# A hybrid block on one core: the front in three groups instead of two, with selection issued between mixing, and other limits for the sparse gathers

## The chip, the cores and the metric

The kernel runs on one core of a Trainium2 chip. The metric is the device time of one execution in microseconds; less is better. Five engines work beside each other, each in the order of its own instruction stream: TensorE (PE; its weight loads are listed as PEld), VectorE (DVE), ScalarE (ACT), GpSimd (POOL) and SyncE (SP), which here only issues transfers.

## What is computed

1024 tokens of width 1024 in float32 pass through one block:

```python
xn = rmsnorm(x, attn_norm_g);  proj = xn @ w_in                  # 1024 -> 2560
b, c, hc = proj[:, :512], proj[:, 512:1024], proj[:, 1024:1536]
z = gelu(proj[:, 1536:]);      u, v = z[:, :512], z[:, 512:]
y_conv = b * causal_conv3(c * hc, conv_w)
y_sgu  = u * (masked w_s @ group_rmsnorm(v) + b_s)               # in blocks of 128 tokens
h = x + concat(group_rmsnorm(y_conv), group_rmsnorm(y_sgu)) @ w_out
hn = rmsnorm(h, ffn_norm_g);   q = hn @ w_q                      # 8 heads x 2 halves x 128
s = q . sub_keys                                                 # 128 scores per half
top 16 of each half -> 256 sums -> top 16 of 128*128 experts per head, softmax gates
h = h + sum over the 8*16 chosen: gate * gelu(peer_u[i] . hn) * peer_v[i]
out = rmsnorm(h, final_norm_g)
```

## The kernel before, in words

The 1024 tokens are eight tiles of 128. Tiles 0 to 3 (S_TILES) get the chosen experts by gathering their rows; tiles 4 to 7 (D_TILES) multiply by all 16384 experts and weight the result with a gate matrix that is zero but at the chosen ones. A Tile scheduler fixes the order of the instructions of each engine when the program is built, by data dependences, the order in which the code issues them, and its own estimates of durations; on the chip each engine follows that order. The parts are:

- **Mixing** (`prep`, `mix`), once for tiles 0 to 3 (group A) and once for 4 to 7 (group B). Every product with a weight matrix is a call of `wide` (L226): a 1024 x 128 slice of weights is loaded by SP (`wraw`, two buffers), split by ACT (`wh`, L169) and DVE (`wl`, L170) into a high and a low part, and 24 matmuls of 128x512 (L179 to L181) follow. Mixing has 28 such calls per group (20 for `w_in`, 8 for `w_out`). It ends with the rows of h and hn in DRAM and with the transposed hn in the tiles `Xh` and `Xl`, in which the transposed x stood before.
- **Selection** (`query`, `choose`): 16 calls of `wide` per group for `w_q`, the scores (L372), and on DVE the searches for 16 largest values (`top16`, L470 to L474) and the comparisons that turn positions into expert numbers (L426 to L430). POOL adds up candidate numbers (`cidx`, L404). For group A it also makes the lists of rows to gather (`si`).
- **Gates** (`gates`, L538): for the dense tiles, 64 blocks of one-hot products: DVE writes one factor, ACT scales the other (L556), PE multiplies, ACT copies to a staging tile (L567), SP stores it to `G_dr`.
- **Dense** (`Dense`): 32 groups of four chunks of 128 experts. `up` (L580) is 24 matmuls with `peer_uT` and a Gelu into a tile of `ring`; `run` (L592) then multiplies the ring tile by the gates (`w`, L606, on DVE) and issues 32 products with `peer_v` (L620). The ring has RING = 4 tiles: three groups of `up` are ahead, twelve calls in all, issued between the gates (L670). The products of three of eight halves go through PSUM at once and are added on DVE (L624).
- **Sparse** (`sparse`, L494): 1024 slots. In a slot POOL gathers 128 rows of 4 KB (L506) into one of NGX = 6 buffers `gx`; DVE then uses them, either for a dot product (L513, `peer_u`) or for a scaled sum (L522, `peer_v`). The code issues sparse last, but the scheduler may place a slot wherever its data are ready. `pace` (L489) holds it back: the first NFREE = 150 slots are free, each later slot has to come after a certain point of the dense loop (its `marks` are the L606 and L624 instructions), spread evenly.

The order in which the main code issues the front is: mixing of A; selection of A; mixing of B; selection of B; gates and the first twelve `up`; then the dense loop:

```python
    prep(A); mix(A)
    qa = query(A, ...); ca = [choose(A, part) for part in A.parts]   # two tiles a part
    ...
    load_x(B); prep(B); mix(B)
    ...
    for c in range((RING - 1) * CB):
        dn.up(c, ps, "pp", 4)
        take(gg, 64 // ((RING - 1) * CB))
```

(`take(gen, n)` advances a generator by n of its steps.)

Of the kernel before, what the change touches and what calls it, by code (L numbers as in the profile page):

```python
# [36 lines left out]

S_TILES = [0, 1, 2, 3]
# [9 lines left out]
NGX = 6  # L48
RING = 4
# [6 lines left out]
NFREE = 150  # L56
# [7 lines left out]
def block_kernel(ctx: ExitStack, tc: tile.TileContext, x, attn_g, w_in, conv_w, sgu_wT, sgu_b, sgu_g,  # L64
# [18 lines left out]
    pre = ExitStack()  # L83
    ps = pre.enter_context(tc.tile_pool(name="ps", bufs=4, space=PSUM))
# [126 lines left out]
    def transposed(G, srcs, gcol):  # L211
        hi, lo = G.dest
        for k in range(KC):
            pt = ps.tile([P, G.T], F32, name="pt", bufs=4)
# [5 lines left out]

    def prep(G):
        xr = G.xr
        scaled(G, xr)
        transposed(G, xr, g_attn)

    def wide(G, src, col, rh, rl, order=tuple(range(KC))):  # L226
        wh, wl = wslice(src, col)
# [4 lines left out]

    def mix(G):
        T, nt, tiles = G.T, G.nt, G.tiles
        xTh, xTl = G.dest
        c2 = ExitStack()
        py = sb(c2, f"py{G.t0}")
        yTh = py.tile([P, KC, T], F32R, name="yTh")
        yTl = py.tile([P, KC, T], F32R, name="yTl")
        with ExitStack() as c3:  # L240
            wk = sb(c3, f"wk{G.t0}", 2)

            def proj(col):
                return wide(G, w_in, col, xTh, xTl)

            def token_rstd(ys, sm, width):
                o = ps.tile([P, nt, 8], F32, name="pt", bufs=4)
                for g in range(4):
                    sq = wk.tile([P, T], F32, name="sq", bufs=1)
                    a_.activation(sq, ys[g], AF.Square)  # L250
                    for j in range(nt):
                        pe.matmul(o[:, j, :], sq[:, j * P:(j + 1) * P], sm[:, g, :], start=g == 0 and j == 0,
                                  stop=g == 3, skip_group_check=True)
                r = wk.tile([P, nt, 8], F32, name="gr", bufs=2)
                a_.activation(r, o, AF.Sqrt, bias=eps, scale=1.0 / width)
                v_.reciprocal(r, r)
                return r

            def group_norms(ys, sm, width):
                r = token_rstd(ys, sm, width)  # L260
                o = ps.tile([8, T], F32, name="pt", bufs=4)
                for j in range(nt):
                    pe.transpose(o[:, j * P:(j + 1) * P], r[:, j, :], ident)
                rh = wk.tile([8, T], F32R, name="ct", bufs=CTB)
                a_.activation(rh, o, AF.Copy)
                rl = wk.tile([8, T], F32R, name="ct", bufs=CTB)
                v_.tensor_tensor(rl, o, rh.bitcast(F32), ALU.subtract)
                for g in range(4):
                    o = ps.tile([P, T], F32, name="pt", bufs=4)
                    pe.matmul(o, selT[:, g, :], rh, start=True, stop=False)  # L270
                    pe.matmul(o, selT[:, g, :], rl, start=False, stop=True)
                    v_.tensor_tensor(ys[g], ys[g], o, ALU.mult)

            def to_yT(k, yn, gcol):
                a_.activation(yTh[:, k, :], yn, AF.Copy, scale=gcol)
                v_.scalar_tensor_tensor(yTl[:, k, :], yn, gcol, yTh[:, k, :].bitcast(F32),
                                        op0=ALU.mult, op1=ALU.subtract)

            vtok = [r.rearrange("p (j g c) -> p j g c", j=2, g=4) for r in rows((nt + 1) // 2)]
            vs, us, cs = [], [], []  # L280
            for g in range(4):
                vt = wk.tile([P, T], F32, name="yk", bufs=4)
                a_.activation(vt, proj(2048 + g * P), AF.Gelu)
                vs.append(vt)
            vr = token_rstd(vs, selA, P)
            for g in range(4):
                vn = vs[g]
                a_.activation(vn, vn, AF.Copy, scale=g_sgu[:, g:g + 1])
                pt = ps.tile([P, nt, P], F32, name="pt", bufs=4)
                for j in range(nt):  # L290
                    pe.transpose(pt[:, j, :], vn[:, j * P:(j + 1) * P], ident)
                for j in range(nt):
                    a_.activation(vtok[j // 2][:, j % 2, g, :], pt[:, j, :], AF.Copy, scale=vr[:, j, 2 * g:2 * g + 1])
            for g in range(4):
                wsT = wk.tile([P, P], F32, name="wsT")
                nc.sync.dma_start(wsT, sgu_wT[:, g, :])
                v_.memset(wsT[64:128, 0:64], 0.0)
                bs = wk.tile([1, P], F32, name="bs")
                nc.sync.dma_start(bs, sgu_b[:, g, :])
                ut = wk.tile([P, T], F32, name="yk", bufs=4)  # L300
                a_.activation(ut, proj(1536 + g * P), AF.Gelu)
                o = ps.tile([P, T], F32, name="pt", bufs=4)
                for j in range(nt):
                    sl = slice(j * P, (j + 1) * P)
                    pe.matmul(o[:, sl], vtok[j // 2][:, j % 2, g, :], wsT, start=True, stop=False)
                    pe.matmul(o[:, sl], ones, bs, start=False, stop=True)
                v_.tensor_tensor(ut, ut, o, ALU.mult)
                us.append(ut)
            group_norms(us, selA, P)
            for g in range(4):  # L310
                to_yT(4 + g, us[g], g_os[:, g:g + 1])
            for g in range(4):
                ct = wk.tile([P, T], F32, name="ct", bufs=CTB)
                a_.activation(ct, proj(512 + g * P), AF.Copy)
                z = wk.tile([P, T + 2], F32, name="z", bufs=1)
                v_.tensor_copy(z[:, 0:2], carry[:, g, :])
                v_.tensor_tensor(z[:, 2:], ct, proj(1024 + g * P), ALU.mult)
                v_.tensor_copy(carry[:, g, :], z[:, T:T + 2])
                cv = wk.tile([P, T], F32, name="yk", bufs=4)
                a_.activation(cv, z[:, 0:T], AF.Copy, scale=cw[:, 0, g:g + 1])  # L320
                v_.scalar_tensor_tensor(cv, z[:, 1:T + 1], cw[:, 1, g:g + 1], cv, op0=ALU.mult, op1=ALU.add)
                v_.scalar_tensor_tensor(cv, z[:, 2:T + 2], cw[:, 2, g:g + 1], cv, op0=ALU.mult, op1=ALU.add)
                v_.tensor_tensor(cv, cv, proj(g * P), ALU.mult)
                cs.append(cv)
            group_norms(cs, selB, 64)
            for g in range(4):
                to_yT(g, cs[g], g_oc[:, g:g + 1])

            hs = rows(nt)
            for j, t in enumerate(tiles):  # L330
                nc.sync.dma_start(hs[j], x[t * P:(t + 1) * P, :])
            for c in range(KC):
                ot = wk.tile([P, T], F32, name="ct", bufs=CTB)
                a_.activation(ot, wide(G, w_out, c * P, yTh, yTl, (4, 5, 6, 7, 0, 1, 2, 3)), AF.Copy)
# [387 lines left out]
```

## Time and profile before

| | |
|---|---|
| median of 3 runs | 2960.36 us (2956.91 to 2960.62) |
| the profiled execution | 2950.23 us, of which its span (first to last instruction) is 2948.5 us |
| PE busy | 2491.7 us, 85% of the span |
| DVE busy | 2278.2 us, 77% |
| POOL busy | 1372.4 us, 47% |
| ACT busy | 794.3 us, 27% |
| mean granted clock of TensorE | 0.912 of 2.4 GHz |
| moved by DMA | 817.26 MB, 277 GB/s over the span |

Shares of busy time are means over stages that have different limits. The stages are told apart by the first and last instruction of a line: the selection of A starts with the first L470 at 238 us, that of B with the next run of L470 at 709 us, the gates with the first L547 at 928 us, the dense loop with the first L606 at 1201 us, and the last of the 32 L606 stands at 2800 us. The table of stretches by engine is cut at these places.

### The profile page before, as it was taken

How to read it: one execution, taken by the hardware profiler on the slowest of the kernel's cores; microseconds unless marked ns; L12 is line 12 of the kernel's file. 1: busy time of each engine (PE TensorE's matmuls, PEld its weight loads, DVE VectorE, ACT ScalarE, POOL GpSimd, SP SyncE). 2: the span in 40 equal slices, each digit the busy share in tenths (PEclk: the TensorE clock that was granted, in tenths of full speed). 3: DMA queues.
4: the chain of work that ended last, by engine and by line, in shares of the span. 5: the costliest groups of instructions: out<-in, count | busy, mean ns of one | idle time of the engine just before them, and what ended most of it. 6: DMA issues, size and time to landing. Idle time of an engine off the chain costs nothing.

```text
span 2948.5 us, 29181 instructions
## 1 busy us (share of the span) xinstructions
PE 2491.7 (85%) x9120; PEld 1916.8 (65%) x9120; DVE 2278.2 (77%) x4500; ACT 794.3 (27%) x1312; POOL 1372.4 (47%) x1383
## 2 busy tenths in 40 slices
PE   8986647995467898889989989998998998899886
PEld 6874436874355777666767667766766766677664
DVE  3349998788999765588778767877777786787778
ACT  5233223233125999211111111111111112111101
POOL 0002225553222100476665656676566666666665
PEclk9998878897688999999999999999999999999998
DMA  3224227786232765999999999999999999999988
GB/s 125 86 96 159 95 67 258 265 302 244 78 96 90 230 188 157 369 394 369 363 351 366 354 349 358 352 371 365 350 345 358 367 354 342 368 362 371 332 310 329
DMA packets 281964, 817.26 MB, mean 277 GB/s; under 512 B 25032, under 2 KB 95696, under 8 KB 277712
## 3 DMA queue, kind: packets, MB, share of 16 engines
q0 software_dynamic: 147456, 536.94, 49.6%
q1 hardware_dynamic: 134352, 278.45, 26.3%
q8 instruction: 72, 1.18, 0.2%
q14 instruction: 84, 0.69, 0.1%
HBM read 771.25 MB, written 44.04 MB: 277 GB/s over the span
## 4 chain that ended last, share of the span: by engine, by line
issue 41%; POOL 17%; DVE 16%; PE 14%; DMA 11%; ACT 0%; POOLq 0%; SPq 0%; DVEq 0%; ACTq 0%
POOL gx L506 17%; DMA gx<-peer_v,si 8%; PE pp L181 3%; PE pp L179 3%; PE pp L180 3%; DMA gx<-peer_u,si 2%; DVE idx L430 2%; DVE acc L522 1%; DVE gx L513 1%; DVE sel L429 1%; DVE s L472 1%; DVE ti L474 1%; DVE ti L471 1%; DVE wl L170 1%; DVE tv L470 1%
## 5 line engine op out<-in xcount | busy, mean ns | idle before, releaser
L506 POOL DMA_INDIRECT gx<-peer_v,si x512 | 627.1, 1225 | 647.8 <-DVE acc L522 454.8
L506 POOL DMA_INDIRECT gx<-peer_u,si x512 | 684.8, 1337 | 485.3 <-DVE dots L513 275.9
L522 DVE SCALAR_TENSOR_TENSOR acc<-gx,dots,acc 128x1024 f32<-128x1024 f32 x512 | 658.0, 1285 | 127.7 <-DMA gx<-peer_v,si 117.9
L513 DVE CUSTOM_DVE_ANT_0 gx<-gx,hn 128x1024 f32<-128x1024 f32 x512 | 613.8, 1222 | 171.8 <-DMA gx<-peer_u,si 168.6
L620 PE MATMUL pa<-v,ring 128*128 128x512 f32 x1280 | 565.0, 592 | 0.0
L181 PE MATMUL pu<-Xh,ul 128*128 128x512 f32 x928 | 391.9, 422 | 127.7 <-DVE ul L170 127.7
L620 PEld LDWEIGHTS pa<-v,ring 128*128 128x128 f32 x1280 | 394.6, 308 | 154.8
L169 ACT ACTIVATE uh<-uraw 128x1024 fp32r<-128x1024 f32 x128 | 135.3, 1058 | 1077.3 <-PE pu L180 1048.3
L179 PE MATMUL pu<-Xh,uh 128*128 128x512 f32 x928 | 397.1, 428 | 11.9 <-ACT ring L590 7.7
L180 PE MATMUL pu<-Xl,uh 128*128 128x512 f32 x928 | 383.0, 413 | 0.0
L181 PE MATMUL pp<-Xh,wl 128*128 128x512 f32 x576 | 237.4, 414 | 150.6 <-DVE wl L170 150.6
L620 PE MATMUL pv<-v,ring 128*128 128x512 f32 x768 | 348.6, 597 | 15.4 <-DVE ac L624 15.4
L181 PEld LDWEIGHTS pu<-Xh,ul 128*128 128x128 f32 x928 | 188.7, 203 | 182.6 <-DVE ul L170 140.0
L620 PEld LDWEIGHTS pv<-v,ring 128*128 128x128 f32 x768 | 234.0, 309 | 107.5 <-DVE ac L624 21.1
L179 PE MATMUL pp<-Xh,wh 128*128 128x512 f32 x576 | 239.9, 417 | 5.3 <-ACT wh L169 4.0
L404 POOL TENSOR_TENSOR cidx<-i,i 128x16 f32<-128x16 f32 (+3 forms) x224 | 40.2, 210 | 425.2 <-ACT i L394 425.0
L180 PE MATMUL pp<-Xl,wh 128*128 128x512 f32 x576 | 237.8, 413 | 0.0
L170 DVE TENSOR_TENSOR ul<-uraw,uh 128x1024 fp32r<-128x1024 f32 x128 | 156.2, 1222 | 105.0 <-ACT uh L169 79.3
L181 PEld LDWEIGHTS pp<-Xh,wl 128*128 128x128 f32 x576 | 115.1, 200 | 177.3 <-DVE wl L170 152.8
L179 PEld LDWEIGHTS pu<-Xh,uh 128*128 128x128 f32 x928 | 188.9, 204 | 56.3 <-ACT ring L590 8.6
L180 PEld LDWEIGHTS pu<-Xl,uh 128*128 128x128 f32 x928 | 187.3, 202 | 49.9 <-issue 6.7
L565 PE MATMUL pt<-og,o 128*128 128x128 f32 x1024 | 185.0, 318 | 20.1 <-ACT og L556 19.3
(181 smaller groups left out, 2860.7 us busy)
## 6 DMA issues: line engine op xcount, KB each, us to landing
uraw<-peer_uT SPq DMA_DIRECT2D x128, 512.0 KB, 5.8
v<-peer_v SPq DMA_DIRECT2D x128, 512.0 KB, 10.1
G_dr<-stg SPq DMA_DIRECT2D x16, 2048.0 KB, 10.0
G<-G_dr SPq DMA_DIRECT2D x32, 1024.0 KB, 7.4
wraw<-w_in SPq DMA_DIRECT2D x40, 512.0 KB, 4.3
wraw<-w_q SPq DMA_DIRECT2D x32, 512.0 KB, 4.2
xt<-x SPq DMA_DIRECT2D x16, 512.0 KB, 5.3
wraw<-w_out SPq DMA_DIRECT2D x16, 512.0 KB, 4.6
```

The source lines that it names most:

```text
L169: a_.activation(hi, raw, AF.Copy)
L170: v_.tensor_tensor(lo, raw, hi.bitcast(F32), ALU.subtract)
L179: pe.matmul(o, lh, rh, start=first, stop=False)
L180: pe.matmul(o, lh, rl, start=False, stop=False)
L181: pe.matmul(o, ll, rh, start=False, stop=last)
L404: eng.tensor_tensor(dst[:, :, c:c + n], second[:, :, b0:b0 + n], first[:, :, a0:a1].to_broadcast([P, nt, n]), ALU.add)
L430: v_.tensor_reduce(part.idx[:, :, h, k0:k0 + 8], sel.rearrange("p j c k -> p j k c"), axis=AX.X, op=ALU.add)
L506: gp_.indirect_dma_start(out=gx, out_offset=None, in_=tab, in_offset=bass.IndirectOffsetOnAxis(ap=ii[:, s:s + 1], axis=0))
L513: pace(v_.tensor_tensor_reduce(gu, gu, hn, 1.0, 0.0, ALU.mult, ALU.add, dots[:, s:s + 1]), slot[0])
L522: pace(v_.scalar_tensor_tensor(acc, gv, dots[:, s:s + 1], acc, op0=ALU.mult, op1=ALU.add), slot[0])
L565: pe.matmul(o[:, i, :], o2[:, m, :], og[:, m, :], start=True, stop=True)
L620: pe.matmul(o, w[:, j * P:(j + 1) * P, m], vs[m][:, dh * 512:(dh + 1) * 512], start=m == 0 and (loose or g == 0), stop=m == CB - 1 and (lo ...
```

## The change

- **Three groups.** A is tiles 0 and 1, B tiles 2 and 3, C tiles 4 to 7. A and B are 256 tokens wide, so that their matmuls, evictions and vector instructions on [128, T] tiles have 256 columns; C has 512 as before. A and B hold their x each in one half of `Xh` and `Xl`, and their transposed hn in a tile of the new pool `yp`. The weights of mixing and selection are now loaded and split three times instead of two.
- **Issue order.** `mix` is a generator with 22 steps. After the mixing of A, each step of the mixing of B is followed by two steps of A's `query`, and every second one by a step of A's `choose`; the same with C and B. C's own selection is issued alternately with the first `up` calls. The gates come after all of it and have none in between.
- **Limits.** RING 4 to 5 (16 `up` calls ahead instead of 12), NGX 6 to 5, NFREE 150 to 400. In `query`, `q` has one buffer instead of two and `s` two instead of three. The junk tile of `scaled` shares the buffer of `sq`.

The body of `mix` is otherwise the same, with `yield` after each slice.

```diff
+GROUPS = [[0, 1], [2, 3], [4, 5, 6, 7]]
-NGX = 6
-RING = 4
+NGX = 5
+RING = 5
-NFREE = 150
+NFREE = 400
...
+    pq = sb(tks, "pq")
+    yp = sb(front, "yp")
+    wk = sb(front, "wk", 2)
+    xt = sb(front, "xt")
...
-    A, B = Group(S_TILES, X), Group(D_TILES, X)
-    A.parts = [Part(dk, 0, 2), Part(dk, 2, 2)]
-    B.parts = [Part(dk, 0, 2), Part(dk, 2, 2)]
+    A, B, C = Group(GROUPS[0], 0), Group(GROUPS[1], 1), Group(GROUPS[2])
+    A.parts = [Part(dk, 0, 2)]
+    B.parts = [Part(dk, 0, 2)]
+    C.parts = [Part(dk, 0, 2), Part(dk, 2, 2)]
...
-            q = pq.tile([P, T], F32, name="q", bufs=2)
+            q = pq.tile([P, T], F32, name="q", bufs=1)
...
-            s = pq.tile([P, nt, P], F32, name="s", bufs=3)
+            s = pq.tile([P, nt, P], F32, name="s", bufs=2)
...
+    def picks(G):
+        q, chs = query(G), [choose(G, part) for part in G.parts]
+        for h in range(NH):
+            take(q, 1)
+            yield
+            take(q, 1)
+            yield
+            for ch in chs:
+                take(ch, 1)
+        take(q)
+        for ch in chs:
+            take(ch)
...
+    take(mix(A))
+    for G, F in ((B, A), (C, B)):
+        load_x(G)
+        q, ch = query(F), choose(F, F.parts[0])
+        for i, _ in enumerate(mix(G)):
+            take(q, 2)
+            if i % 2:
+                take(ch, 1)
+        take(ch)
+    front.close()
+    rx = ExitStack()
+    dn = Dense(sb(rx, "ringp", side="right"), sb(rx, "uvp", side="right"))
+    nup = (RING - 1) * CB
+    for i, _ in enumerate(picks(C)):
+        if i < nup:
+            dn.up(i, ps, "pp", 4)
+    for part in C.parts:
+        spread(C, part)
...
         gg = gates(sb(c1, "gp"), D_TILES, 0, NTB, OGP)
-        for c in range((RING - 1) * CB):
-            dn.up(c, ps, "pp", 4)
-            take(gg, 64 // ((RING - 1) * CB))
         take(gg)
```

**Place 1: DVE, in the selection of A.** `wl` is a split of weights, `s` and `cand` are searched, `sel` and `idx` are positions, `gx` a sparse slot, `yk` a product of mixing. Before, the piece holds selection, splits of `w_q` and a slot:

```order
L426 TENSOR_TENSOR eq<-iota_c,posf 128x800
L429 TENSOR_TENSOR sel<-eq,cidx 128x2x160
L444 TENSOR_REDUCE den<-gt 128x4
L430 TENSOR_REDUCE idx<-sel 128x2x8
L445 RECIPROCAL den<-den 128x4
L170 TENSOR_TENSOR wl<-wraw,wh 128x1024
L429 TENSOR_TENSOR sel<-eq,cidx 128x800
```

With the change a split and a gating product of B's mixing (L325, 256 columns) stand between A's searches:

```order
L494 MAX tv<-s 128x8 x2
L495 MAX_INDEX ti<-tv,s 128x8 x2
L194 TENSOR_TENSOR wl<-wraw,wh 128x1024
L325 TENSOR_TENSOR yk<-yk,pt 128x256
L451 TENSOR_REDUCE idx<-sel 128x2x8
L447 TENSOR_TENSOR eq<-iota_c,posf 128x800
L492 MAX_INDEX pos<-top,cand 128x8
L450 TENSOR_TENSOR sel<-eq,cidx 128x800
```

The mixing of B has moved from behind A's selection to between its instructions.

**Place 2: DVE, the end of the gates.** L553 and L547 (L574 and L568 with the change) are factors of the gates, L606 (L627) the first product of the dense loop. Before:

```order
L553 TENSOR_TENSOR o_8747<-iota_r,dTb 128x1024
L547 TENSOR_TENSOR o_8721<-iota_k,dT 128x1024
L559 TENSOR_SCALAR og<-iota_k,dT 128x128 x8
L547 TENSOR_TENSOR o_8744<-iota_k,dT 128x1024
L170 TENSOR_TENSOR ul<-uraw,uh 128x1024 x4
L606 TENSOR_TENSOR ring<-ring,G 128x2048
```

With the change:

```order
L574 TENSOR_TENSOR o_10568<-iota_r,dTb 128x1024
L543 SCALAR_TENSOR_TENSOR acc<-gx,dots,acc 128x1024
L534 ISA gx,dots<-gx,hn 128x1024
L534 ISA dots 128x1
L568 TENSOR_TENSOR o_10590<-iota_k,dT 128x1024
L580 TENSOR_SCALAR og<-iota_k,dT 128x128 x8
L568 TENSOR_TENSOR o_10613<-iota_k,dT 128x1024
L574 TENSOR_TENSOR o_10616<-iota_r,dTb 128x1024
```

Slots (L534, L543) now stand between the gates up to their end; before, the last third of the gates had none.

**Place 3: DVE, the end of the program.** L533 (L554) adds h to the last sparse rows, L624 and L636 (L645 and L657) add up dense products, L481 (L502) scales a finished row. Before:

```order
L636 TENSOR_TENSOR v<-v,pa_8789 128x512
L636 TENSOR_TENSOR v<-v,pa_8790 128x512
L522 SCALAR_TENSOR_TENSOR acc<-gx,dots,acc 128x1024 x2
L186 RECIPROCAL frs<-frs 128x1
L522 SCALAR_TENSOR_TENSOR acc<-gx,dots,acc 128x1024
L481 SCALAR_TENSOR_TENSOR v<-v,frs,uraw 128x1024
L522 SCALAR_TENSOR_TENSOR acc<-gx,dots,acc 128x1024 x2
L533 TENSOR_TENSOR acc<-acc,gx 128x1024
```

With the change:

```order
L543 SCALAR_TENSOR_TENSOR acc<-gx,dots,acc 128x1024 x4
L554 TENSOR_TENSOR acc<-acc,gx 128x1024
L645 TENSOR_TENSOR ac_10651<-ac_10651,pv 128x512
L210 RECIPROCAL frs<-frs 128x1
L502 SCALAR_TENSOR_TENSOR acc<-acc,frs,gx 128x1024
L210 RECIPROCAL frs<-frs 128x1
L657 TENSOR_TENSOR v<-v,pa_10656 128x512
L502 SCALAR_TENSOR_TENSOR ac_10651<-ac_10651,frs,uraw 128x1024
```

Before, the last sparse slot stood behind the last dense addition; with the change it stands ahead of the last L645 and of all L657.

## Rows read from the trace of the kernel before

**Rows 1.** Table of stretches by stage: us, busy us (and instructions) of each engine
```profile
core 0: us, PE busy (x) PEld busy (x) DVE busy (x) ACT busy (x) POOL busy (x), PEclk, DMA share, GB/s
0.00:238.00 238.00, 216.80 (x1015) 176.49 (x1016) 100.75 (x196) 95.49 (x142) 0.88 (x7) 0.95 0.31 107
238.00:452.00 214.00, 109.20 (x495) 85.78 (x493) 213.09 (x1072) 55.00 (x117) 54.25 (x193) 0.77 0.29 98
452.00:705.00 253.00, 224.10 (x973) 178.75 (x974) 207.99 (x317) 84.99 (x124) 139.66 (x103) 0.86 0.81 294
705.00:928.00 223.00, 125.89 (x555) 99.64 (x554) 222.60 (x1074) 55.04 (x120) 51.74 (x192) 0.76 0.25 82
928.00:1186.00 258.00, 233.44 (x1273) 189.67 (x1272) 174.60 (x270) 245.61 (x538) 28.31 (x21) 0.93 0.64 189
...
2800.50:2948.50 148.00, 110.92 (x254) 77.51 (x252) 118.29 (x122) 8.73 (x17) 89.53 (x72) 0.90 0.87 320
```

**Rows 2.** The same table, cut at the first and the fifth L606
```profile
0.00:1201.10 1201.10, 924.52 (x4373) 742.72 (x4374) 922.71 (x2930) 542.29 (x1044) 274.83 (x515) 0.86 0.48 161
...
1273.20:2800.50 1527.30, 1397.09 (x4312) 1051.91 (x4312) 1180.92 (x1382) 233.05 (x241) 963.56 (x764) 0.95 0.96 359
```

**Rows 3.** Line L606: duration ns min/median/max, first and last start us
```profile
L606 DVE TENSOR_TENSOR ring<-ring,G x32: 2278/2285/2293, 1201.1 to 2800.5; 128x2048 f32<-128x2048 f32 x32
```

**Rows 4.** Timeline of DVE, the fifth L606: start us, us
```profile
1273.19 2.28 DVE L606 TENSOR_TENSOR ring<-ring,G 128x2048 f32<-128x2048 f32 x1
```

**Rows 5.** Stretches, line L522 alone (one instruction a slot): us, DVE busy (x)
```profile
0.00:1201.10 1201.10, 69.11 (x54) 0.86 0.48 161
...
1273.20:2800.50 1527.30, 493.81 (x384) 0.95 0.96 359
```

**Rows 6.** Stretches, line L513 alone (two instructions a slot): us, DVE busy (x)
```profile
0.00:1201.10 1201.10, 115.13 (x192) 0.86 0.48 161
...
1273.20:2800.50 1527.30, 456.64 (x758) 0.95 0.96 359
```

**Rows 7.** Instructions that use wraw: duration ns min/median/max, first and last start
```profile
L169 ACT ACTIVATE wh<-wraw x88: 1040/1061/1182, 13.7 to 875.5; 128x1024 fp32r<-128x1024 f32 x88
L170 DVE TENSOR_TENSOR wl<-wraw,wh x88: 1194/1222/1243, 14.8 to 877.5; 128x1024 fp32r<-128x1024 f32 x88
```

**Rows 8.** DMA issues: KB each, median us from issue to landing
```profile
wraw<-w_in SPq DMA_DIRECT2D x40, 512.0 KB, 4.3
```

**Rows 9.** Timeline of PE at the first scores of A: start us, us
```profile
235.97 0.39 PE L179 MATMUL pp<-Xh,wh 128*128 128x512 f32 x1
236.19 0.39 PE L180 MATMUL pp<-Xl,wh 128*128 128x512 f32 x1
236.42 1.14 PE L372 MATMUL pt<-key,q 128*128 128x128 f32 x8
237.32 0.47 PE L181 MATMUL pp<-Xh,wl 128*128 128x512 f32 x1
```

**Rows 10.** Costliest groups of ACT, 928 to 1186 us: busy us, mean ns
```profile
L556 ACT ACTIVATE og<-o,dT 128x128 f32<-128x128 bf16 x384 | 169.5, 535 | 0.0
L567 ACT ACTIVATE stg<-pt 128x512 f32<-128x512 f32 x128 | 76.4, 608 | 7.3 <-PE pt L565 5.9
```

**Rows 11.** Instructions that use gx, whole span: waits (us, times) and landing times
```profile
  DVE acc L522: 499.3, 149
...
  DMA gx<-peer_u,si: 168.6, 150
...
DMA to landing us min/median/max: 4.2/7.1/13.8
```

**Rows 12.** Stretch of the last four groups of L620: us, PE busy (x)
```profile
2799.00:2922.70 123.70, 112.27 (x256) 78.64 (x256) 0.96 0.91 330
```

**Rows 13.** Costliest groups of the page: busy us, mean ns
```profile
L620 PE MATMUL pa<-v,ring 128*128 128x512 f32 x1280 | 565.0, 592 | 0.0
```

**Rows 14.** Instructions that use gx, 2800.5 to 2948.5 us: the sparse rows' finish
```profile
L533 DVE TENSOR_TENSOR acc<-acc,gx x1: 1225/1225/1225, 2940.4 to 2940.4; 128x1024 f32<-128x1024 f32 x1
```

More of the change, by code (lines that the diff above doesn't have):

```diff
@@ L234, in mix @@
         T, nt, tiles = G.T, G.nt, G.tiles
[L235 to L261, printed above, removed]
-                for j in range(nt):
[L263 to L280, printed above, removed]
-            for g in range(4):
[L282 to L301, printed above, removed]
-                o = ps.tile([P, T], F32, name="pt", bufs=4)
[L303 to L334, printed above, removed]
-                pt = ps.tile([P, nt, P], F32, name="pt", bufs=4)
-                for j in range(nt):
-                    pe.transpose(pt[:, j, :], ot[:, j * P:(j + 1) * P], ident)
-                cc = slice(c * P, (c + 1) * P)
-                for j in range(nt):
-                    v_.tensor_tensor(hs[j][:, cc], hs[j][:, cc], pt[:, j, :], ALU.add)
@@ L341, in mix, with proj, token_rstd @@
-        c2.close()
+        prep(G)
+        yield
+        def proj(col):
+            return wide(G, w_in, col, G.x)
+        def token_rstd(ys, sm, width):
+            o = ps.tile([P, nt, 8], F32, name="pt", bufs=4)
+            for g in range(4):
+                sq = wk.tile([P, T], F32, name="sq", bufs=1)
+                a_.activation(sq, ys[g], AF.Square)
+                for j in range(nt):
+                    pe.matmul(o[:, j, :], sq[:, j * P:(j + 1) * P], sm[:, g, :], start=g == 0 and j == 0,
+                              stop=g == 3, skip_group_check=True)
+            r = wk.tile([P, nt, 8], F32, name="gr", bufs=2)
+            a_.activation(r, o, AF.Sqrt, bias=eps, scale=1.0 / width)
+            v_.reciprocal(r, r)
+            return r
@@ new lines, in to_yT @@
+        def to_yT(k, yn, gcol):
+            hi, lo = G.y[0][k], G.y[1][k]
+            a_.activation(hi, yn, AF.Copy, scale=gcol)
+            v_.scalar_tensor_tensor(lo, yn, gcol, hi.bitcast(F32), op0=ALU.mult, op1=ALU.subtract)
+        vtok = [r.rearrange("p (j g c) -> p j g c", j=2, g=4) for r in rows((nt + 1) // 2)]
+        vs, us, cs = [], [], []
+        for g in range(4):
+            vt = wk.tile([P, T], F32, name="yk", bufs=4)
+            a_.activation(vt, proj(2048 + g * P), AF.Gelu)
+            vs.append(vt)
+            yield
@@ new lines, in mix @@
+        group_norms(cs, selB, 64)
+        for g in range(4):
+            to_yT(g, cs[g], g_oc[:, g:g + 1])
+        hs = rows(nt)
+        for j, t in enumerate(tiles):
+            nc.sync.dma_start(hs[j], x[t * P:(t + 1) * P, :])
+        for c in range(KC):
+            ot = wk.tile([P, T], F32, name="ct", bufs=CTB)
+            a_.activation(ot, wide(G, w_out, c * P, G.y, (4, 5, 6, 7, 0, 1, 2, 3)), AF.Copy)
+            pt = ps.tile([P, nt, P], F32, name="pt", bufs=4)
+            for j in range(nt):
+                pe.transpose(pt[:, j, :], ot[:, j * P:(j + 1) * P], ident)
+            cc = slice(c * P, (c + 1) * P)
+            for j in range(nt):
+                v_.tensor_tensor(hs[j][:, cc], hs[j][:, cc], pt[:, j, :], ALU.add)
+            yield
```

129 lines of the change are left out of this document (87 added, 42 removed).

## The prediction

> **What bounds the kernel now.** I read the page first (busy shares, the slices, the chain), then the table of stretches, because the shares of the whole span hide that the stages have different limits. The table [rows 1] shows it: in the two selections DVE is busy 213 of 214 and 223 of 223 us while PE has half its time free, at a granted clock of 0.77; in the mixing of A PE has 217 of 238 us and DVE only 101; in the gates ACT has 246 of 258. So the front has two kinds of stage that need different engines, one after the other. Up to the first L606 at 1201.1 us [rows 3] DVE is busy 922.7 us [rows 2]: 278 us of it are idle, 137 in the mixing of A, 45 in that of B, 83 in the gates. That is all an interleaved front can win.
>
> The dense loop is another matter. From the fifth L606 at 1273.2 [rows 4] to the last at 2800.5 [rows 3] its 27 periods take 1527.3 us, 56.6 each, with a DMA share of 0.96 at 359 GB/s [rows 2]. PE alone would need 50 us: four `up` calls of 24 matmuls, which follow each other every 0.225 us [rows 9], are 21.6, and the 64 products 64 x 565.0/1280 = 28.3 [rows 13]. The transfers bound it. A period has 384 + 758/2 = 763 slots over 27, that is 28.3 [rows 5, 6]. It also loads 5.24 MB of tables and gates, 14.6 us at 359 GB/s, which leaves (56.6 - 14.6)/28.3 = 1.485 us for a slot. POOL stood 499 us until DVE freed a gather's buffer, and DVE 169 us until a gather landed [rows 11].
>
> **The order, before any cost.** The scheduler's order on DVE tells how many slots stand ahead of each dense multiplication. Before, 150 stood ahead of the first (54 + 192/2) [rows 5, 6]. With the change it is 177, not 400: the limit is lifted, but the front has no room in the scheduler's eyes. After that the slots before the fifth, and before the last multiplication are 193 and 948. Of the 27 periods between, 21 carry 26 to 31 slots (640 together) and six 15 or 20. Before, it was 28 nearly everywhere. So the loop is loaded less evenly.
>
> **Mixing of A alone.** Half as many columns, the same 28 slices. Eight 128-column matmuls take 0.90 us (236.42 to 237.32), 0.113 each [rows 9], so a 256-column one costs between 0.113 and 0.225; I take 0.12, as the streaming halves, or 2.9 us a slice instead of 5.4. Then the slice's own loop binds: landing 4.3 [rows 8], ACT 1.06, DVE 1.22 [rows 7], 6.6 us over two buffers, 3.5 with the handovers. The stage is 238 - 28 x 1.9 for the slices, less half of the other 217 - 151 = 66 us of PE work: 152 us.
>
> [...] In this trace PE fell to 0.77 where it was half idle [rows 1]; no row has a 256-column matmul. [...]
>
> **The mixed stages.** DVE's work up to the first multiplication is 922.7, plus 44 more splits of 1.22 [rows 7] (54 us), four more `up` splits (5), 27 more slots at (69.1 + 115.1)/150 = 1.23 [rows 5, 6] (33), and about 5 for the fixed part of twice as many half-width instructions: 1019 us. Of this about 65 fall to the mixing of A. C's selection, half of the two old ones [rows 1] without the 34 slots that the order put there, with 16 `up` splits and 20 slots, is 242. The gates (174.6 [rows 1] without ten splits and 22 slots, plus the 60 slots that the order now puts there) are 212. That leaves 500 us for the two mixed stages. PE needs less there (A's selection with B's mixing 44 x 2.9 + 33 = 161, B's with C's mixing about 265), so DVE bounds them. The question is how full it gets. In the old selections it was full; in the mixing of B, with slots filled in, it was busy 208 of 253, 82% [rows 1], because instructions of a chain (split, matmul, eviction, normalisation) stand in its fixed order and block what is ready behind them. The mixed stages are of both kinds, and I take the middle, 91%: 549 us, with 500 and 610 as ends. C's selection takes 243.
>
> **Gates.** ACT bounds them: 245.6 us [rows 1], nearly all in L556 and L567 [rows 10], less about 21 for the ten `up` calls that left, is 224, at the old 95% 235 us, and again 15 to the first multiplication. The 60 slots on DVE are hidden under ACT; should they not be, DVE's 212 us are still below. The first L606 then comes at 152 + 549 + 243 + 250 = 1194, against 1201: the overlap wins back idle time and the 44 extra splits, the worse-filled pipeline and the extra slots spend it. Ends: 1145 and 1255.
>
> **Dense loop.** Four multiplications and 16 slots, about 35 us, lead to the fifth. Then the 21 full periods are bound by transfers, 21 x 14.6 + 640 x 1.485 = 1257, and the six others by PE, 6 x 50 = 300: 1557, against 1527 and a first stretch of 72, so some 7 us less in sum. The 27 slots that left the loop should be worth 40; the uneven load eats most of it, since in the six light periods the transfers wait for PE.
>
> **Five gather buffers.** A slot every 2.00 us over six buffers means that one buffer's round takes 12.0 us: landing (median 7.1 [rows 11]), DVE, the wait for its turn and for POOL. The full periods now ask for a slot every 59.9/30.5 = 1.96 us, so a round of 9.8. If no part of the round shrank, a slot would take 2.40 and 640 slots cost 282 us more; if the landing shrinks with fewer gathers in flight, nothing. The landing is 4.2 at best and 7.1 at the median, so much of it is queueing, and the DMA share of 0.96 says that the transfers and not the buffers bind. I stay near the low end and take 0.05 a slot, 30 us; ends 0 and 282, the upper far less likely.
>
> **End.** With RING 5 the last L606 is four groups ahead of PE instead of three, so five groups of products follow it. The last four took 123.7 [rows 12], 30.9 each; five are 155, and the last row's addition, norm and store 8 (2940.4 [rows 14] to the end at 2948.5). That is 163 against 148 [rows 1], and the order agrees: the sparse rows now finish ahead of the dense ones. Ends 148 and 175.
>
> **Sum.** 1194 + 35 + 1557 + 30 + 163 = 2979, against a span of 2948.5: 30 us more. The profiled execution took 2950.2 us, so about 2981 by its like; the median of the runs lies 10 us above it, and the forecast for it is 2960.4 + 30.5 = 2991 us, 1% slower.
>
> **The cases.** About 0.2% (6 us) is what a measurement can tell from no change.
>
> 1. *Slightly to clearly slower, as summed* (2967 to 3040, at 2991): chance 0.39.
> 2. *The front packs* and the time is faster. Place: DVE between the end of A's mixing and C's. If it is busy 99% there, the stages take 505 instead of 549 and the first multiplication comes at 1150; if also five buffers carry the transfers, and the last five groups run at 28.3, the sum is 1150 + 35 + 1557 + 149 = 2891, 57 less: 2903. For it speaks that selections ran DVE at 99%, that DVE always has searches that wait for nothing, and that a large part of the old idle time (137 + 45 us) stood beside work that could have filled it. Against it speaks the 82%. From a fill of about 96%, with no cost of the buffers, it is faster. Chance 0.32.
> 3. *Nothing measurable*: the two effects cancel, between 2954 and 2966. Chance 0.12.
> 4. *The narrow slices do not get cheaper*, by their own speed or by the lower clock. Then A's mixing stays at 205, A's selection with B's mixing is bound by PE (44 x 5.4 + 33 = 271 instead of some 209), and B's with C's gains about 20: 135 more than the forecast, 3126. Against it: 0.113 for 128 columns. Chance 0.06.
> 5. *The buffers bind*: 2.15 us a slot in the full periods, (2.15 - 1.96) x 640 = 122 instead of 30: 3083. For it: DVE waits for landings already with six. Chance 0.11.
>
> **Numbers.** Faster is case 2, 0.32; same case 3, 0.12; slower cases 1, 4 and 5, 0.56. As cases of both signs hold much, the likeliest one's own range is 2967 to 3040; the range that should hold 8 in 10 goes from 2912, leaving out the best part of case 2, to 3075, leaving out case 4 and the worse half of case 5.
>
> **What would show it.** In the new profile: L205, L203 and L204 with 256 columns starting every 0.12 us, or not; the first L627 near 1194 and 177 slots ahead of it; DVE busy about 91% between 150 and 700 us; a gate stage near 235 us with ACT at 95%; periods of L627 near 60 to 61 us where 31 slots stand in them and 50 where 20 do; the landing median below 7.1 and POOL waiting longer for DVE than before; five groups of products after the last L627 and dense rows that finish last. The prediction is wrong if the first L627 comes before 1160 or after 1240, or if full periods are shorter than 59 or longer than 65 us.

## The result and the profile after

The changed kernel takes **3076.2 us** (median; 3073.1 to 3088.0) against 2960.5 beside it: a ratio of **1.0398, interval 1.0368 to 1.0428**, 116 us slower. The forecast was 2991, and its range ended at 3075. The profiled execution is the longest of the four (3087.95, span 3086.2). The table of stretches of the changed kernel, cut at its own stages (columns as in [rows 1]):

```profile
150.00:700.00 550.00, 458.70 (x2659) 398.72 (x2658) 489.72 (x1494) 235.39 (x409) 186.88 (x282) 0.88 0.63 215
700.00:942.00 242.00, 201.43 (x895) 162.56 (x893) 242.00 (x1095) 88.21 (x152) 58.02 (x195) 0.93 0.31 102
942.00:1197.00 255.00, 204.66 (x1029) 168.96 (x1030) 194.77 (x303) 231.24 (x517) 59.80 (x46) 0.83 0.72 218
1226.80:1270.70 43.90, 38.07 (x84) 23.55 (x85) 32.62 (x42) 1.29 (x2) 20.38 (x16) 0.83 1.02 412
1270.70:2686.70 1416.00, 1199.31 (x3604) 874.62 (x3603) 1042.52 (x1203) 201.77 (x209) 895.18 (x676) 0.93 0.93 341
2686.70:2913.00 226.30, 207.04 (x640) 156.28 (x639) 131.03 (x161) 31.02 (x31) 108.24 (x80) 0.95 0.76 267
2913.00:3086.20 173.20, 143.28 (x318) 97.30 (x316) 119.18 (x121) 8.51 (x17) 89.30 (x71) 0.93 0.78 279
```

Its dense multiplications:

```profile
L627 DVE TENSOR_TENSOR ring<-ring,G x32: 2280/2284/2294, 1226.8 to 2913.0; 128x2048 f32<-128x2048 f32 x32
```

Against [rows 1 to 4]: the first multiplication comes at 1226.8 instead of 1201.1 (+25.7), the first to the fifth take 43.9 instead of 72.1 (-28.2), the fifth to the last 1642.3 instead of 1527.3 (**+115.0**), the rest 173.2 instead of 148.0 (+25.2): 137.7 in all. The -28.2 and much of the +25.2 come with RING = 5, which puts the first long period behind the fifth multiplication instead of ahead of it, and one more group of products behind the last (42.2 and 196.9 us in e3, below). So the loss is in the loop, and there DMA is less busy than before (0.93 against 0.96), and in the last four periods, with 20 slots each, only 0.76. What PE waited for between 1400 and 2400 us, before (first) and after:

```profile
PE pu L181 <- DVE ul L170: 77.3, 18, 6.5
PE pv L620 <- DVE ac L624: 0.9, 1, 0.9
```
```profile
PE pu L205 <- DVE ul L194: 88.1, 15, 7.9
PE pv L641 <- DVE ac L645: 58.5, 23, 4.3
```

The second wait is new: the products of the loose rows stand until DVE has added the previous one (L645), and DVE's order has slots ahead of that addition. It comes with the limit: over the same 1000 us it is 32 us in e1, 6 in e2 and 65 in e9, below.

### The profile page after: what moved, and what is told of

It reads as the page before. It is cut to its first block, busy times and chain, and to the rows that moved or that the text cites. A ratio compares the mean times of both kernels' runs of the same rounds, so it can differ in the third digit from the quotient of the medians.

```text
span 3086.2 us, 31824 instructions
## 1 busy us (share of the span) xinstructions
PE 2600.5 (84%) x10192; PEld 2016.1 (65%) x10192; DVE 2345.3 (76%) x4615; ACT 882.6 (29%) x1478; POOL 1434.9 (46%) x1383
## 3 DMA queue, kind: packets, MB, share of 16 engines
q1 hardware_dynamic: 143720, 303.36, 28.7%
## 5 line engine op out<-in xcount | busy, mean ns | idle before, releaser
L527 POOL DMA_INDIRECT gx<-peer_v,si x512 | 659.5, 1288 | 525.1 <-DVE acc L543 367.0
L543 DVE SCALAR_TENSOR_TENSOR acc<-gx,dots,acc 128x1024 f32<-128x1024 f32 x512 | 658.1, 1285 | 212.0 <-DMA gx<-peer_v,si 196.6
L534 DVE CUSTOM_DVE_ANT_0 gx<-gx,hn 128x1024 f32<-128x1024 f32 x512 | 616.3, 1222 | 249.2 <-DMA gx<-peer_u,si 246.6
L641 PE MATMUL pv<-v,ring 128*128 128x512 f32 x768 | 392.8, 659 | 113.1 <-DVE ac L645 103.5
L203 PE MATMUL pu<-Xh,uh 128*128 128x512 f32 x896 | 382.3, 427 | 4.2 <-ACT ring L611 3.5
L586 PE MATMUL pt<-og,o 128*128 128x128 f32 x1024 | 203.4, 350 | 49.5 <-ACT og L577 49.0
L586 PEld LDWEIGHTS pt<-og,o 128*128 128x128 f32 x1024 | 168.1, 234 | 84.9 <-ACT og L577 60.9
L205 PE MATMUL pp<-Xh,wl 128*128 128x256 f32 (+1 forms) x608 | 211.9, 349 | 12.2 <-DVE wl L194 12.2
L425 POOL TENSOR_TENSOR cidx<-i,i 128x16 f32<-128x16 f32 (+3 forms) x224 | 60.2, 298 | 336.8 <-ACT i L415 292.7
L203 PE MATMUL pp<-Xh,wh 128*128 128x256 f32 (+1 forms) x608 | 212.3, 349 | 3.7 <-ACT wh L193 3.7
L204 PE MATMUL pp<-Xl,wh 128*128 128x256 f32 (+1 forms) x608 | 209.7, 345 | 0.0
L194 DVE TENSOR_TENSOR wl<-wraw,wh 128x1024 fp32r<-128x1024 f32 x132 | 160.6, 1220 | 46.7 <-ACT wh L193 46.2
```

The lines of the kernel that those rows point to most:

```text
L194: v_.tensor_tensor(lo, raw, hi.bitcast(F32), ALU.subtract)
L203: pe.matmul(o, lh, rh, start=first, stop=False)
L204: pe.matmul(o, lh, rl, start=False, stop=False)
L205: pe.matmul(o, ll, rh, start=False, stop=last)
L425: eng.tensor_tensor(dst[:, :, c:c + n], second[:, :, b0:b0 + n], first[:, :, a0:a1].to_broadcast([P, nt, n]), ALU.add)
L527: gp_.indirect_dma_start(out=gx, out_offset=None, in_=tab, in_offset=bass.IndirectOffsetOnAxis(ap=ii[:, s:s + 1], axis=0))
```

## Experiments

### The four parts, each alone

```diff
e1 (before)   -NFREE = 150    +NFREE = 400
e2 (before)   -NGX = 6        +NGX = 5
e3 (before)   -RING = 4       +RING = 5
e4 (changed)  -NGX = 5, RING = 5, NFREE = 400    +NGX = 6, RING = 4, NFREE = 150
```

> The kernel before with NFREE = 400 alone. In the scheduler's order 185 slots stand ahead of the first dense multiplication instead of 150, then about 31 in each of 18 periods and 20 in each of the last seven. Theory U (uneven load: a period of about 56 us holds 28 slots for nothing, and costs 2 us for every further one, while one with 20 is no shorter than 56): 18 to 20 periods at 62 to 63 instead of 56.6, light ones at 55 to 56.5, 3050 to 3080 us. Theory B (the five gather buffers are what made the periods long): with six buffers 31 slots take 60, the light periods 50 to 52, 2950 to 2985 us. Reckoning of the prediction (transfers bind, 14.6 us and 1.485 us a slot, light periods 50): 31 slots 60.6, 20 slots 50, 2960 to 2980 us.

> The kernel before with NGX = 5 alone; 28 slots a period as before. Theory B: the buffers bind, 2.2 to 2.4 us a slot, periods of 60 to 66, 3050 us or more. Theory U: transfers and the chain of PE and DVE set 56 to 58 us, 2960 to 3000 us. Reckoning of the prediction: 0.05 us a slot, 2990 us.

> The kernel before with RING = 5 alone. All theories: one more group of products behind the last multiplication (148 becomes 165 to 175 from it to the end) and one period less ahead of it, with four up calls more ahead of the first one (10 to 25 us later). Theory U: the periods stay at 56 to 57, 2960 to 2985 us. A rival, R, in which the fifth group is worth its buffer because PE never waits for the multiplications: PE's wait at L203 to L205 and L620 falls and the time is 2900 to 2950 us.

> The changed kernel with NGX = 6, RING = 4 and NFREE = 150, so the front in three groups alone. 150 slots stand ahead of the first dense multiplication and 28 in a period, as before. Theory U and theory B both hold that the loop and the end take what they took before, so the whole difference is when the first multiplication starts. By the profile of the changed kernel (1226.8 with 27 more slots and four more up calls) that is 1180 to 1215 us, and the time 2940 to 2975 us. Theory F (the front itself costs the 25 us, whatever the numbers are): first multiplication at 1220 to 1235, 2980 to 2995 us. Reckoning of the prediction: 2925 to 2960 us.

| run | us | ratio (interval) | first multiplication | fifth to last |
|---|---|---|---|---|
| e1 limit 400 | 2964.6 | 1.0026 (1.0005 to 1.0048) | 1215.5 | 1542.5 |
| e2 five buffers | 3031.8 | **1.0234** (1.0205 to 1.0263) | 1204.9 | 1589.5 |
| e3 RING 5 | 2970.3 | 1.0022 (1.0000 to 1.0045) | 1216.0 | 1516.7 |
| e4 front alone | 2975.8 | 1.0045 (1.0022 to 1.0067) | 1212.3 | 1539.3 |

Theory U, my own at that point, is refuted twice: 31 slots with six buffers take 59.3 us (19 periods of e1), not 62 to 63, and five buffers lengthen a period that has only 28, by 2.3 us (1589.5 / 27 = 58.9). Theory B is right in its direction; its 60 to 66 us a period and 3050 us were too much, and the prediction's own reckoning, 2990 us, was 42 too low. e4 comes out 1 us above the range of theories U and B and 4 below that of theory F: its first multiplication is 11 us later than before, its loop 12 us longer. In e3 the end grew to 196.9 us, more than all theories said: the order leaves 106 slots behind the last multiplication there, 78 before. The four ratios together make 3.3%, not 4.0: some 20 us must come from parts that meet.

### How many buffers

```diff
e5 (before)   -NGX = 6    +NGX = 7
e6 (before)   -NGX = 6    +NGX = 4
e10 (before): ten buffers from slot 256 on
+NGY = 4
+GYFROM = 256
+                if slot[0] >= GYFROM and slot[0] % (NGX + NGY) >= NGX:
+                    gx = more.tile([P, D], F32, name="gy", bufs=NGY)
+                else:
+                    gx = pool.tile([P, D], F32, name="gx", bufs=NGX)
```

> The kernel before with NGX = 7 alone. Theory B (how many gathers are in flight sets the slots' pace; five cost 71 us against six) with a round that shrinks as the queues empty: less and less for each further buffer, 20 to 45 us off, 2915 to 2940 us. Theory T (with six the transfers bind, DMA share 0.96, and a seventh gather only waits longer in the queues): within 6 us of before, and the gathers' landing grows. Theory U would see no change either.

> The kernel before with NGX = 4 alone. Theory B: the cost grows faster than evenly, 150 to 300 us over before, 3110 to 3260 us, with a DMA share of 0.8 to 0.9 in the loop. Theory S (a fixed part of the slot's round was lost by one buffer less, for instance the end of each tile, which borrows two gather buffers): another 60 to 75 us on the 71 of five buffers, 3090 to 3107 us.

> The kernel before with four more gather buffers from slot 256 on, in memory that is free once the gates are done (NGX = 6, then 10 in turn). The slots a period stay at 28. Theory T2 (at seven buffers the transfers are nearly full, DMA share 0.97, so more gathers in flight mostly land later): landing 9 us or more, periods 53 to 55, 2870 to 2915 us. Theory B to its end (every wait of the loop came from the buffers): periods at PE's 50, 2760 to 2820 us.

(`more` is a pool opened beside the loop's own.) Seven: **2916.4 us, 0.9847** (0.9810 to 0.9884). Four: **3212.6, 1.0837** (1.0798 to 1.0876). Ten: 2880.4, 0.9715 (0.9672 to 0.9758). Between 1400 and 2400 us (columns as in [rows 1]) four, five, six (the kernel before), seven and ten buffers give, each from its own run:

```profile
1400.00:2400.00 1000.00, 829.71 (x2458) 601.13 (x2457) 680.81 (x800) 137.50 (x143) 561.79 (x437) 0.92 0.88 313
```
```profile
1400.00:2400.00 1000.00, 888.13 (x2723) 667.29 (x2723) 745.22 (x888) 148.58 (x155) 620.14 (x479) 0.94 0.94 345
```
```profile
1400.00:2400.00 1000.00, 914.03 (x2824) 689.47 (x2823) 769.55 (x910) 153.80 (x160) 629.92 (x498) 0.95 0.96 358
```
```profile
1400.00:2400.00 1000.00, 928.57 (x2886) 699.27 (x2885) 788.78 (x926) 156.37 (x162) 634.44 (x509) 0.96 0.97 366
```
```profile
1400.00:2400.00 1000.00, 942.45 (x2966) 712.25 (x2964) 800.08 (x945) 160.92 (x166) 653.92 (x521) 0.97 0.98 376
```

The gathers of u there (last number: median us from issue to landing), with four, five, six and seven buffers:

```profile
gx<-peer_u,si POOLq DMA_INDIRECT x224, 6.1
```
```profile
gx<-peer_u,si POOLq DMA_INDIRECT x256, 6.8
```
```profile
gx<-peer_u,si POOLq DMA_INDIRECT x256, 6.9
```
```profile
gx<-peer_u,si POOLq DMA_INDIRECT x256, 7.8
```

A period takes 64.6, 58.9, 56.6, 55.3 and 54.3 us with 4, 5, 6, 7 and 10 buffers. A gather lands only 0.1 to 0.9 us sooner for each buffer less, so what is taken away is not made good. Theory B holds at both ends (four buffers cost about 180 us more than five, and not the 60 to 75 more of theory S; a seventh gains 45, where theory T saw nothing). Ten come out in T2's range, but not for its reason: 376 GB/s is not all that the transfers give (394 in the full periods of e11, below), while seven of the 27 periods already take 49.5 us, the time that PE needs by itself.

### Parts that meet

```diff
e7 (changed)   -NGX = 5, RING = 5    +NGX = 6, RING = 4
e8 (changed)   -NFREE = 400    +NFREE = 150
e9 (before)    -NGX = 6, NFREE = 150    +NGX = 5, NFREE = 400
e11 (before)   -NGX = 6, NFREE = 150    +NGX = 7, NFREE = 400
```

> The changed kernel with NGX = 6 and RING = 4: the front in three groups and NFREE = 400. The order has 183 slots ahead of the first dense multiplication, 31 or 32 in most periods and 20 in the last seven. If the parts add (+3 for the limit, +15 for the front): 2975 to 2985 us. If the 20 us that the four parts leave unexplained in the whole change lie between front and limit (more slots in the front, whose gathers stand in a stage that has no time for them): 2990 to 3005 us.

> The changed kernel with NFREE = 150, so front, five buffers and RING = 5; 28 slots a period. If the unexplained 20 us lie between the limit and the five buffers (31 slots a period cost more with five buffers than the light periods give back): 3045 to 3060 us. If they lie between RING = 5 and the five buffers, or in the front: 3065 to 3080 us.

> The kernel before with NGX = 5 and NFREE = 400; front and ring as before. The order has 181 slots ahead of the first dense multiplication, 31 in most periods, 20 in the last six. Theory BL (the two numbers meet: five buffers give a slot every 2.04 to 2.06 us at best, so 31 slots can't be had in less than 63 us): 3065 to 3085 us, full periods at 63 to 64. Theory A (the numbers add, 71 + 3, and the other 40 of the changed kernel come from the front or RING = 5): 3025 to 3045 us, full periods at 60 to 61.

> The kernel before with NGX = 7 and NFREE = 400. Theory BL: with seven buffers a slot can come every 1.85 us or less, so 31 slots take 57 to 58 and the last eight periods, with 20, 50 to 51; with 39 more slots ahead of the first multiplication (14 us later) and a shorter end, 2900 to 2925 us, no worse than seven buffers alone (2916). Theory A: 2920 to 2930 us.

e7: 2972.6 us, 1.0037 (1.0013 to 1.0061). e8: 3030.1, 1.0218 (1.0178 to 1.0259). e9: **3089.3, 1.0424** (1.0373 to 1.0475). e11: **2880.9, 0.9730** (0.9677 to 0.9782). e9, with the old front and ring, already has the whole loss; e8, with everything but the limit, costs no more than five buffers alone. So the loss is made by **two numbers that meet**: the raised limit costs 57 us with five buffers (e9 against e2), 3 with six (8 by the ratio), and gains 36 with seven. e7 comes 2 us below the range of adding parts, e9 4 us above the end of theory BL, e8 15 us below both theories' ranges, and e11 19 us below BL's. Why e8 costs some 25 us less than e2, e3 and e4 added up is open. With the raised limit, the full periods of e1, and the full and light ones of e9 and of e11:

```profile
1286.90:2413.60 1126.70, 1000.29 (x3043) 741.63 (x3041) 902.31 (x1060) 169.25 (x176) 772.68 (x592) 0.95 0.98 370
```
```profile
1301.10:2554.60 1253.50, 1077.13 (x3202) 780.06 (x3201) 939.88 (x1109) 177.37 (x184) 794.38 (x613) 0.93 0.94 345
2613.60:2950.90 337.30, 310.58 (x960) 234.53 (x959) 198.51 (x234) 47.62 (x48) 158.92 (x120) 0.95 0.77 273
```
```profile
1291.60:2342.80 1051.20, 973.85 (x3039) 721.75 (x3038) 895.53 (x1058) 169.72 (x176) 772.51 (x589) 0.98 1.01 394
2391.70:2739.40 347.70, 345.90 (x1120) 263.01 (x1119) 231.02 (x266) 56.17 (x57) 171.45 (x140) 1.00 0.85 310
```

The full stretches are 19, 20 and 19 periods. Against 28 slots a period, a further slot costs 1.6 us with five buffers (58.9 us at 28.3 slots in e2, 62.7 at 30.7 in e9), 1.0 with six (56.6 at 28.3 before, 59.3 at 31.1 in e1) and nothing with seven (55.3 at 28.2 in e5, 55.3 at 30.9 in e11).

Six light periods take 56.2 us each with five buffers, seven take 49.7 each with seven, where PE is busy 345.9 of 347.7 us. But 20 slots at 2.05 are 41 us: why is a light period long? DVE's timeline of one of the changed kernel, and of one of e11 (idle time in brackets):

```profile
2804.27 6.56 DVE L543 SCALAR_TENSOR_TENSOR acc<-gx,dots,acc 128x1024 f32<-128x1024 f32 x5
2810.75 0.68 DVE L645 TENSOR_TENSOR ac<-ac,pv 128x512 f32<-128x512 f32 x1
2811.35 1.28 DVE L543 SCALAR_TENSOR_TENSOR acc<-gx,dots,acc 128x1024 f32<-128x1024 f32 x1
2813.28 1.28 DVE L543 SCALAR_TENSOR_TENSOR acc<-gx,dots,acc 128x1024 f32<-128x1024 f32 x1 [0.65 <-DMA gx<-peer_v,si]
...
2831.20 1.28 DVE L543 SCALAR_TENSOR_TENSOR acc<-gx,dots,acc 128x1024 f32<-128x1024 f32 x1 [3.21 <-DMA gx<-peer_v,si]
...
2839.30 2.60 DVE L543 SCALAR_TENSOR_TENSOR acc<-gx,dots,acc 128x1024 f32<-128x1024 f32 x2 [1.15 <-DMA gx<-peer_v,si]
2841.82 2.35 DVE L194 TENSOR_TENSOR ul<-uraw,uh 128x1024 fp32r<-128x1024 f32 x2
```
```profile
2593.04 6.56 DVE L522 SCALAR_TENSOR_TENSOR acc<-gx,dots,acc 128x1024 f32<-128x1024 f32 x5
2599.52 0.68 DVE L624 TENSOR_TENSOR ac<-ac,pv 128x512 f32<-128x512 f32 x1
2600.12 6.56 DVE L522 SCALAR_TENSOR_TENSOR acc<-gx,dots,acc 128x1024 f32<-128x1024 f32 x5
...
2620.20 1.28 DVE L522 SCALAR_TENSOR_TENSOR acc<-gx,dots,acc 128x1024 f32<-128x1024 f32 x1 [0.45 <-DMA gx<-peer_v,si]
2622.08 1.23 DVE L170 TENSOR_TENSOR ul<-uraw,uh 128x1024 fp32r<-128x1024 f32 x1 [0.59 <-ACT uh L169]
```

The 20 slots stand in a row, between the loose additions and ahead of the splits. With five buffers the first six run without a stop and the rest mostly at the pace of the gathers: 38 us to the split at 2841.8. For such splits PE waits 19.3 us in the last four periods. With seven the row ends after 29 us, and the split waits for ACT's half instead.

### The front, and joining what carries

```diff
e13 (changed, with the numbers of e4)
-    for i, _ in enumerate(picks(C)):
-        if i < nup:
-            dn.up(i, ps, "pp", 4)
+    take(picks(C))
...
         gg = gates(sb(c1, "gp"), D_TILES, 0, NTB, OGP)
+        for c in range(nup):
+            dn.up(c, ps, "pp", 4)
+            take(gg, 64 // nup)
e12 (changed): RING = 4, NFREE = 150, buffers as in e10 but 5 + 4
e14 (changed): RING = 4, NFREE = 150, buffers as in e10, 6 + 4
e15 (before): NFREE = 400, buffers as in e10 but 7 + 3
e16 (e13 with NFREE = 400, 6 buffers + 2 from slot 190 on)
```

> The changed kernel with NGX = 6, RING = 4, NFREE = 150 as in e4, and the up calls back among the gates, four gate blocks' steps between two of them, as before; two of them still come to stand in the selection, as before. Theory G (the gates take 248 us with or without them, since they rode there for nothing; in C's selection, where DVE has no idle time, ten of them cost ten splits of 1.22 us and more): gates begin at 928 to 932 instead of 942, the first multiplication at 1198 to 1205, 2955 to 2967 us. Rival (ACT binds the gates, so the ten calls' conversions and activations lengthen them by 15 to 25 us again): first multiplication at 1210 to 1222, 2970 to 2985 us.

> The changed kernel with RING = 4, NFREE = 150 and four more gather buffers from slot 256 on (five, then nine in turn): the front in three groups with a loop that does not lack buffers. If the front costs the same 10 to 15 us whatever the loop does, it stands that much above the kernel before with ten buffers: 2885 to 2930 us. If the front's few microseconds vanish behind a loop that waits less, it equals that kernel within 6 us.

> The changed kernel with RING = 4, NFREE = 150, six gather buffers and four more from slot 256 on: the front in three groups beside e10, whose front is the old one. If the front costs its 11 us at the first multiplication and little else: 2885 to 2905 us. If the 50 us between e12 and e10 were the front's and not those of five buffers ahead of slot 256 and nine behind it: 2920 to 2940 us.

> The kernel before with NGX = 7, three more gather buffers from slot 256 on, and NFREE = 400. Theory T2 (in e11 the transfers are full at 392 GB/s and a share of 1.00 where 31 slots stand, and the light periods are PE's 49.5): nothing left for buffers to win in either, 2865 to 2890 us. Theory B to its end: 10 to 40 us less than e11's 2881, 2840 to 2870 us.

> The front in three groups with its up calls among the gates, NGX = 6, two more gather buffers from slot 190 on, RING = 4, NFREE = 400. If the front's 10 us carry over and eight buffers do what seven do in e11 (2881 us, ratio 0.973): ratio 0.965 to 0.971. If the front gives nothing in a loop that the transfers bind, because slots that the front did not take come back in the loop: 0.972 to 0.978.

e13: 2957.3 us, **0.9966** (0.9945 to 0.9988), 23 us less than e4 by the ratios. At the first multiplication the profiles show 8 of them (1203.9 against 1212.3); where the rest arises they do not show, since e13's is that of its longest execution. The gate stage, from its first comparison to its last eviction, before, in e4 and in e13:

```profile
928.20:1181.60 253.40, 228.92 (x1253) 185.93 (x1251) 173.17 (x269) 244.43 (x538) 28.31 (x21) 0.93 0.63 189
```
```profile
942.00:1193.40 251.40, 204.51 (x1027) 172.19 (x1027) 170.38 (x271) 230.04 (x516) 34.50 (x27) 0.81 0.62 185
```
```profile
936.20:1185.70 249.50, 228.93 (x1248) 182.48 (x1247) 179.60 (x280) 242.88 (x534) 32.79 (x28) 0.95 0.70 206
```

Theory G is right that the calls rode among the gates for nothing: the stage takes 253 and 250 us with ten of them (ACT busy 244 and 243) and 251 with none (ACT 230). Its 928 to 932 us for the start was too early (936.2). e12 (2932.9 us, 0.9885, 0.9840 to 0.9929) ends 3 us above its first theory's range, and e14 (2911.0, 0.9794, 0.9749 to 0.9839) between the ranges of its two. By the ratios, 0.9% of e12's distance to e10 goes with five and nine buffers instead of six and ten, and 0.8% with a front that has its calls in the selection; e14's interval touches those of both, so how the parts share it stays open. e15: 2882.1, 0.9717 (0.9677 to 0.9756), no better than e11, as T2 said. e16: **2867.0, 0.9686** (0.9662 to 0.9710): the lowest median of all, below both kernels. Its interval overlaps those of e11 and e15, so the front's own gain there isn't settled.

## Why the prediction was wrong

**The sign was right, the size a quarter.** Against the sum of 2979 for the span, 3086.2 is 107 more: 33 up to the first multiplication, 9 to the fifth, 55 to the last, 10 behind it. Four terms of the sum failed: the gates (20 us too low), the handover to the first multiplication (15), five gather buffers (38) and the light periods (17). None of them is large by itself, and the prediction's two signs of being wrong did not come: the first multiplication at 1226.8 is within 1160 to 1240, and the full periods, 63.1 us, within 59 to 65.

- *Mixing of A, mixed stages*: right. The first search of A stands at 152.4 us (forecast 152), DVE was busy 489.7 of 550 us in the mixed stages (89%, forecast 91), and the gates began at 942 (forecast 944). Case 2, in which the front packs, set its bound at 96% "with no cost of the buffers"; by the prediction's own terms 92% is enough without that cost (500/0.92 = 543, 6 us less than 549), and 96% makes up for its 30 us. The 89% is below both. In A the 256-column matmuls ran as taken at the high clock, and slower at the low one:

```profile
59.80:61.80 2.00, 2.00 (x16) 1.84 (x15) 1.55 (x5) 1.20 (x4) 0.00 (x0) 1.00 0.03 8
65.10:67.30 2.20, 2.20 (x12) 2.20 (x12) 1.89 (x5) 0.00 (x0) 0.00 (x0) 0.50 0.54 151
```
```profile
61.53 0.28 PE L205 MATMUL pp<-Xh,wl 128*128 128x256 f32 x1
61.65 0.28 PE L203 MATMUL pp<-Xh,wh 128*128 128x256 f32 x1
...
65.15 0.41 PE L203 MATMUL pp<-Xh,wh 128*128 128x256 f32 x1
65.36 0.41 PE L204 MATMUL pp<-Xl,wh 128*128 128x256 f32 x1
```

  They start every 0.12 us where the granted clock is 1.00 (2.4 GHz), and every 0.21 where it is 0.50 (1.2 GHz), in a stretch behind two waits for weight splits (1.53 and 0.69 us). The Trainium skill (TensorE: Matmul & The Clock Gate, "Why this matters for your kernels") tells of a swing of the clock for thin matmuls whose loop does not take all blocks of the summed dimension (K) in one go. Here each slice brings all eight of them, so that row does not speak of this loop; the swing shown stands behind waits for splits. Between 150 and 700 us the granted clock was 0.88 in the mean ([rows 1] have 0.77 and 0.86 there), and the start of A's selection was as summed, so no cost of the swing shows that I had not summed.
- *Gates*: "about 21 for the ten `up` calls that left" failed. The stage took 255 us, not 235. ACT lost its work and the stage not its length: in e4 ACT was busy 14.4 us less than before and waited 11.9 us more for PE's products (first row before, then e4: us, times, longest). With the calls back, in e13, that wait is 3.5 us.

```profile
ACT stg L567 <- PE pt L565: 5.9, 11, 0.8
```
```profile
ACT stg L588 <- PE pt L586: 17.8, 37, 0.9
```

- *Handover*: 30 us, not 15. It comes with the raised limit: from the last store of the gates to the first multiplication it is 28.7 to 37.5 us in the seven kernels with NFREE = 400 and 18.2 to 23.9 in the eleven with 150. With the raised limit 10 to 12 slots stand in this stretch, with 150 none. In the changed kernel DMA is busier there, the load of the first gates is issued 21.6 us after that store instead of 10.3, and the first multiplication waits for it. That the slots' gathers hold up the store and the load is likely, but no run shows it by itself. "The 60 slots on DVE are hidden under ACT" asked for DVE's time only. Before, then the changed kernel:

```profile
1181.60:1201.10 19.50, 19.41 (x85) 15.95 (x86) 4.90 (x4) 7.14 (x8) 0.00 (x0) 1.00 0.94 315
```
```profile
1196.60:1226.80 30.20, 22.57 (x96) 17.79 (x96) 14.35 (x22) 7.17 (x7) 16.60 (x13) 0.97 1.03 379
```
```profile
1226.83 2.29 DVE L627 TENSOR_TENSOR ring<-ring,G 128x2048 f32<-128x2048 f32 x1 [7.24 <-DMA G<-G_dr]
```

- *Five gather buffers*: this step failed. "Much of it is queueing" would have let the landing fall by about 2 us with one buffer less (a round of 9.8 us instead of 12.0); it fell by 0.1 to 0.3 for u and v. The round did fall, to 10.4 in e2 (5 x 2.08), by what lay outside the landing. The 0.05 us a slot were too little where 28 slots stand (58.9 - 56.6 = 2.3 us over 28.3 slots, 0.08; e2 as a whole lost 71 us where the term was 30), and more so where the raised limit asks for 31: 62.7 with five (20 periods of e9) against 59.3 with six, 3.4 over 31, 0.11. In the changed kernel 21 full periods took 1325 us, forecast 1257 + 30: 68 for the buffers, 0.11 a slot. That is the mechanism of case 5, with 0.11 too small a chance, but not its price, which was 122 (2.15 us a slot; measured 1325/640 = 2.07). That its 3083 is close to the 3076 is luck: the gates, the handover, the light periods and the end made up the difference.
- *Uneven load*: the six light periods took 317 us, forecast 300 (the five with 20 slots 56.5 each, forecast 50). That PE sets them at 50 is right with seven buffers (49.7); with five, a row of slots ahead of the splits sets them. "The uneven load eats most of it" held in e1: +3 us.
- *The transfers bind the loop* was wrong as the reading of 0.96: with the buffers and the limit of e16 the same table shows 400 GB/s.

```profile
1400.00:2400.00 1000.00, 941.79 (x2941) 696.54 (x2940) 864.33 (x1044) 161.28 (x168) 737.17 (x568) 0.98 1.01 400
```

- *First to fifth multiplication, end*: 44 for 35, and 173 for 163, within its ends; the dense rows finish last, as said. What made these 9 and 10 us is not shown.

## What to carry to other kernels

A busy share of 0.96 does not say that transfers bind: take one gather buffer away and add one, and see whether the landing time follows. Judge a limit on how much side work may stand in a loop together with the buffers that feed it, since the same limit cost 57 us with five and gained 36 with seven. Work that rides for nothing beside a stage's bound engine should stay there; moved into a stage whose engine is full, it is paid for.

## What the runs showed of the hardware beyond that

With ten `up` calls fewer among the gates PE had 226 matmuls less, and its granted clock fell from 0.93 (before) to 0.81 (e4); the median product of the gates then took 377 ns instead of 275, and ACT's wait for them grew as shown above. In e13, with ten calls back, the clock is 0.95 and the product takes 275 ns. And with six buffers more the gathers landed only 3 us later (6.1 with four, 9.1 with ten), while the bytes moved rose from 313 to 376 GB/s.
